# A new order table for a threshold-attention kernel, and one GpSimd drain more

## The chip, the cores and the metric

The kernel runs on one core of a Trainium2 chip. The metric is the device time of one execution in microseconds (us); the time given for a kernel is the median over its runs. A profile is one execution recorded by the hardware profiler, and times within it count from the start of its span.

## The reference

```python
batch, heads, seq, dim = 8, 12, 512, 64          # Q, K, V: float32, threshold 0.1
scores = np.einsum('bhqd,bhkd->bhqk', Q, K) * scale
weights = np.exp(scores - np.max(scores, axis=-1, keepdims=True))
weights = weights / (np.sum(weights, axis=-1, keepdims=True) + 1e-10)
weights = np.where(weights > threshold, weights, 0)
weights = weights / (np.sum(weights, axis=-1, keepdims=True) + 1e-10)
return np.einsum('bhqk,bhkd->bhqd', weights, V)
```

With random inputs nearly every weight is below the threshold, so nearly every row of the output is zero. The kernel makes use of that.

## The kernel before

The output is filled with zeros by 24 large stores (`do_zero`, a *fill* of 512 KB each). The work is to find the few query rows that have a weight above the threshold, and to write those rows.

The 96 heads are taken in 48 pairs, the pairs in 24 *quads*. For a quad, Q and K are loaded (`load_q`, `load_k`), Q is cast to 16 bits (`qcast`, L367 to L371), both are transposed on TensorE (`ktr` L381, `qtr` L410) and taken out of PSUM (`kev` L389/L391, `qev` L416), and K is cast (`kh` L396/L400). Then for each pair and each 128 keys: scores into PSUM (`sc`, L438), an exponential of them (`ex`, on ScalarE L447 or, as a bit trick, on VectorE L449), and sums over keys (`sm`, L468), which give each query two power sums. 384 exponentials of 128x512 run in all. Beside that the squares of Q and K are taken (`bits`, on GpSimd L425, ScalarE L427 or VectorE L429, two steps for a quad) and summed (`norms`, L478): they only serve as a guard, and nothing waits for them but the check at the end.

Pairs form three groups (24, 16 and 8 pairs). When a group's sums are complete, `y`, `d`, `fl` and `mx` on VectorE find the queries whose power sums tell of one large weight. Six *stages* (0 to 5, of 8 pairs; stage 5 is group 2) then finish those queries: `m`, `ix`, `qi` make row numbers; `gq` (L534) gathers the rows of Q by an indirect transfer that GpSimd issues; `xm`, `xev`, `xqk`, `xexp` (L541 to L562) compute their scores again in full precision; `xcut`, `xkeep`, `vi`, `oi` (L566 to L580) find the one key above the threshold; `gv` (L585) gathers that row of V, and `scatter` (L600) writes it to the output. So GpSimd issues 18 indirect transfers: six gq, six gv, six scatters. gv of stage 3 waits for the fills of quads 12 to 23, and each scatter for the fills of its own quads.

Every engine runs its instructions in order. The order is not written out as code: each step is entered in a plan by `add(name, engines, ...)`, and the table `ORDER` lists all 1325 steps as words: the step's number in base 36 and a letter for the engine that takes it (P TensorE, V VectorE, A ScalarE, G GpSimd, S the load queue of SyncE, Q that of ScalarE, N none). `Plan.order` goes through the table and emits each step. A step that has a choice of engines (`ex`, `kev`, `bits`, `xev`, `y`, the casts) takes the one of its letter. Buffers come from pools in the order of the table. The table sets only each engine's own order; at run time an engine waits for data through semaphores. The numbers given to `add` (a cost for each engine, a latency) were used to make such a table and cost nothing on the chip.

Loads and fills are issued on SyncE, at most eight in flight, so a fill stands behind the loads that come before it in the table.

Behind the plan a check counts queries that do not fit the scheme; if there are any, a slow loop (`tc.If(many > 0)`) computes everything in the plain way. With these inputs the branch is not taken. The program ends with a barrier in which each engine drains and SyncE waits for all transfers.

Of the kernel before, what the change touches and what calls it, by code (L numbers as in the profile page):

```python
# [94 lines left out]
def kernel(  # L95
# [18 lines left out]
    nc = tc.nc  # L114
# [391 lines left out]
    def quads_of(x):  # L506
        p0, k = pairs_of_stage(x)
        return range(p0 // 2, (p0 + k) // 2)
# [195 lines left out]
    for g in range(NG):  # L704
# [14 lines left out]
        for x in xs:  # L719
            def xstep(name, engs, lat, after, fn, takes=(), gives=(), mode=None, pr=pr + LAG, x=x):  # L720
                deps = [(a, x) if isinstance(a, str) else a for a in after]
                add((name, x), engs, lat, deps, pr, lambda e: fn(e, x), takes, gives, mode)
# [8 lines left out]
            xstep("xev", {"ACT": 0.3, "DVE": 0.34}, 0.15, ["xm"], do_xev, takes=[("xq", x)],  # L731
                  gives=[("one", ("xm", x))])
            xstep("xqk", {"PE": 1.75}, 0.25, ["xev"], do_xqk, takes=[("one", ("xs", x))],
                  gives=[("xq", x)] + [("big", ("kt", j)) for j in quads_of(x)], mode="c")
            xstep("xexp", {"ACT": 0.7}, 0.12, ["xqk"], do_xexp, takes=[("cut", x)])
            xstep("xcut", {"DVE": 0.15}, 0.04, ["xexp"], do_xcut)
            xstep("xkeep", {"DVE": 0.76}, 0.04, ["xcut"], do_xkeep, gives=[("cut", x), ("one", ("xs", x))])
            xstep("vi", {"DVE": 0.12}, 0.36, ["xkeep"], do_vi)
            xstep("oi", {"DVE": 0.12}, 0.12, ["xkeep", "qf"], do_oi)
            filled = [j for w in range(x, NX) for j in quads_of(w)] if x == NX - 3 else []  # L740
            xstep("gv", {"POOL": 1.25}, 0.1, ["vi"] + [("z", j) for j in filled],
                  lambda e, x, filled=filled: do_gv(e, x, filled), takes=[("vr", x)])
            xstep("scatter", {"POOL": 1.25}, 0.3, ["gv", "oi"] + [("z", j) for j in quads_of(x)], do_scatter)
    bad = consts.tile([P, len(PARTS) + NG + NX], f32)
    nc.vector.memset(bad[:], 0.0)

    NK = len(PARTS)

    def do_check_norm(eng):
        nc.vector.tensor_scalar(bad[:, 0:NK], nmax[:], NORM_CAP / BITS, 0.5, op0=ALU.is_le, op1=ALU.is_lt)  # L750

    def do_check_count(eng):
        for g in range(NG):
            nc.vector.tensor_scalar(bad[HI, NK + g:NK + 1 + g], count[HI, g:g + 1], J * FAR, is_row[HI, g:g + 1],
                                    op0=ALU.is_gt, op1=ALU.mult)
# [19 lines left out]
    Kd, Vd = (t.rearrange("b h (p r) d -> (b h) p (r d)", p=P, r=SO) for t in (K, V))  # L775
    with tc.If(many > 0):
        k_sb, v_sb, q_sb = k_b[0][:, 0, :, 0:D], k_b[1][:, 0, :, 0:D], qs_b[0]
        kt, qt, mt = kt_b[2][0:D, 0, :], kt_b[3][0:D, 0, 0:P], kt_b[4][:, 0, :]
        st, e, m = cut_b[0], kt_b[5][:, 0, :], kt_b[6][:, 0, :]
        with tc.For_i(0, B * H, 1) as hd:  # L780
            nc.sync.dma_start(out=k_sb, in_=Kd[hd].rearrange("p (r d) -> p r d", r=SO))
            nc.sync.dma_start(out=v_sb, in_=Vd[hd].rearrange("p (r d) -> p r d", r=SO))
            for r in range(SO):
                nc.tensor.matmul(one[1][0:D, r * P:(r + 1) * P], lhsT=k_sb[:, r, :], rhs=identity_f32[:],
                                 is_transpose=True, start=True, stop=True)
            nc.scalar.copy(kt, one[1][0:D, :])
            with tc.For_i(0, SO, 1) as r0:
# [58 lines left out]
```

## Time and profile before

| | |
|---|---|
| Median of 3 runs | 172.13 us (171.56 to 172.7) |
| The profiled execution | 173.78 us |
| Its span, first to last instruction | 172.0 us |
| Granted TensorE clock, mean | 0.994 of full |
| Busy in the span: TensorE, VectorE, ScalarE, GpSimd | 160.1, 150.1, 149.4, 130.4 us |
| HBM read and written | 25.56 MB, 12.78 MB |
| Transfers on the load queue of SyncE | 76.1% of 16 DMA engines over the span |

How to read it: busy time is the union of an engine's instructions; register, branch, semaphore and DMA-issuing instructions are not counted. Matmul ends are modelled, so a busy TensorE is not one at its peak. Neighbouring instructions of VectorE, ScalarE and GpSimd overlap by some tens of ns, so a duration is a little longer than the step from one start to the next. An indirect transfer's span on GpSimd is its issue; its data land later.

### The profile page before, as it was taken

The numbers are of one execution on the slowest core, as the hardware profiler recorded it, in microseconds if no ns is written. First come the engines' busy times: TensorE is split into PE (matmuls) and PEld (weight loads), VectorE is DVE, ScalarE is ACT, GpSimd is POOL, SyncE is SP. The second block draws the span as 40 slices with busy tenths as digits, with TensorE's granted clock in tenths as the row PEclk, the third lists the DMA queues.
The fourth block names the chain that finished last, engine by engine and source line by source line (L and its number), as shares of the span: only waits on it lengthen the run. The fifth ranks groups of instructions, "written<-read, shape, count | busy, mean of one in ns | idle before, by whom it ended". The sixth has DMA issues, their size and how long they took to land. (4 is left out here: it accounts for less than half of the span.)

```text
span 172.0 us, 5811 instructions
## 1 busy us (share of the span) xinstructions
PE 160.1 (93%) x2190; PEld 62.7 (36%) x2190; DVE 150.1 (87%) x349; ACT 149.4 (87%) x297; POOL 130.4 (76%) x198
## 2 busy tenths in 40 slices
PE   6598999999999999999999999999999999998950
PEld 2253443443354243434442354334243333332320
DVE  5198999999999999999999999899689999997450
ACT  2577999999999999999999999999899999936720
POOL 8119979999989988960785999799869959536451
PEclk9999999999999999999999999999999999999997
DMA  5999999989899689796998989999899980000000
GB/s 162 263 234 286 238 268 252 278 194 270 184 269 289 143 235 379 166 326 150 226 331 243 320 185 264 360 385 266 268 308 374 398 346 13 1 3 5 6 5 7
DMA packets 67453, 38.27 MB, mean 222 GB/s; under 512 B 51938, under 2 KB 64349, under 8 KB 67424
## 3 DMA queue, kind: packets, MB, share of 16 engines
q1 hardware_dynamic: 64992, 37.10, 76.1%
q10 hardware_dynamic: 1856, 0.66, 1.6%
q8 instruction: 17, 0.28, 0.7%
q0 software_dynamic: 576, 0.13, 0.5%
q14 instruction: 12, 0.10, 0.2%
HBM read 25.56 MB, written 12.78 MB: 223 GB/s over the span
## 5 line engine op out<-in xcount | busy, mean ns | idle before, releaser
L447 ACT ACTIVATE e<-one 128x512 f16<-128x512 f32 x231 | 120.0, 639 | 3.2 <-PE one L438 2.2
L449 DVE TENSOR_SCALAR e<-one 128x512 uint16<-128x512 f32 x153 | 97.0, 683 | 3.3 <-PE one L438 2.9
L438 PE MATMUL one<-big 64*128 64x512 f16 x384 | 67.6, 391 | 1.0 <-ACT big L396 0.5
L468 PE MATMUL sum<-e,w_s 128*32 128x512 f16 (+1 forms) x768 | 59.4, 387 | 0.9 <-ACT e L447 0.7
L425 POOL TENSOR_TENSOR big<-big 128x512 bf16<-128x512 f16 x52 | 52.8, 1038 | 2.3 <-DVE big L429 1.8
L400 POOL CAST big<-big 128x512 f16<-128x512 f32 x47 | 28.2, 613 | 16.3 <-ACT big L389 4.5
L371 POOL CAST qh<-big 128x512 f16<-128x512 f32 x45 | 26.7, 614 | 6.0 <-DMA big<-in_Q_dram 3.0
L438 PEld LDWEIGHTS <-big 64*128 64x128 f16 x384 | 17.2, 97 | 34.5 <-issue 28.1
L468 PEld LDWEIGHTS <-w_s 128*32 128x32 f16 (+1 forms) x768 | 15.9, 95 | 36.1 <-issue 31.5
L389 ACT COPY big<-one 128x512 f32<-128x512 f32 (+1 forms) x37 | 20.5, 591 | 2.7 <-PE one L381 2.6
L416 DVE COPY big<-one 128x512 f16<-128x512 f16 (+1 forms) x52 | 19.5, 398 | 3.3 <-PE one L410 1.2
L381 PE MATMUL one<-identity_f,big 64*128 64x64 f32 x384 | 18.7, 234 | 1.7 <-DMA big<-in_K_dram 1.5
L381 PEld LDWEIGHTS one<-identity_f,big 64*128 64x128 f32 x384 | 16.1, 145 | 6.9 <-issue 3.0
L391 DVE COPY big<-one 128x512 f32<-128x512 f32 (+1 forms) x15 | 9.7, 649 | 3.6 <-PE one L381 3.4
L556 PE MATMUL one<-big,xq 128*32 128x512 f32 x96 | 11.5, 598 | 0.5 <-issue 0.5
L410 PEld LDWEIGHTS <-qh 64*128 64x128 f16 x384 | 9.0, 97 | 7.6 <-issue 3.5
L410 PE MATMUL one<-identity_h,qh 64*128 64x64 f16 x384 | 11.3, 195 | 0.0
L534 POOL DMA_INDIRECT qs<-in_Q_dram,idx x6 | 6.4, 1060 | 6.2 <-DVE idx L524 4.8
L600 POOL DMA_INDIRECT out_dram<-vr,idx x6 | 6.1, 1024 | 4.1 <-DVE cut L566 2.2
L427 ACT ACTIVATE big<-big 128x1024 bf16<-128x1024 f16 x8 | 8.3, 1059 | 0.0
L585 POOL DMA_INDIRECT vr<-in_V_dram,idx x6 | 6.4, 1066 | 2.3 <-DVE idx L575 1.3
L562 ACT ACTIVATE one<-one 128x512 f32<-128x512 f32 x6 | 3.7, 612 | 3.3 <-DVE vals L504 2.0
(83 smaller groups left out, 80.9 us busy)
## 6 DMA issues: line engine op xcount, KB each, us to landing
out_dram<-zero SPq DMA_DIRECT2D x24, 512.0 KB, 6.2
big<-in_K_dram SPq DMA_DIRECT2D x93, 128.0 KB, 4.2
big<-in_Q_dram SPq DMA_DIRECT2D x22, 512.0 KB, 5.5
big<-in_Q_dram SPq DMA_DIRECT2D x3, 256.0 KB
big<-in_K_dram ACTq DMA_DIRECT2D x3, 128.0 KB
big<-in_Q_dram ACTq DMA_DIRECT2D x1, 256.0 KB
qs<-in_Q_dram,idx POOLq DMA_INDIRECT x6
vr<-in_V_dram,idx POOLq DMA_INDIRECT x6, 4.0
```

Source lines behind the costliest of these rows:

```text
L371: behind(nc.gpsimd.tensor_copy(dst, src))
L381: nc.tensor.matmul(dst[i][:, c:c + D], lhsT=src[ps, n0 + n, r, :], rhs=identity_f32[ps, ps], is_transpose=True, start=True, stop=True)
L389: nc.scalar.copy(dst, src)
L400: behind(nc.gpsimd.tensor_copy(dst, src))
L410: nc.tensor.matmul(dst[i][:, c:c + D], lhsT=src[ps, n0 + n, r, :], rhs=identity_h[ps, ps], is_transpose=True, start=True, stop=True)
L416: nc.vector.tensor_copy(qk_b[big("qk", q)][:, 0, n0:n0 + k, i * SO * D:(i + 1) * SO * D], src)
L425: behind(nc.gpsimd.tensor_tensor(out=dst[:, n, :], in0=src[:, n, :], in1=src[:, n, :], op=ALU.mult))
L438: nc.tensor.matmul(one[at("one", ("sc", hp, t, h))][:], lhsT=qk[ps, 1, n, t * P:(t + 1) * P], rhs=qk[ps, 0, n, :], start=True, stop=True)
L447: nc.scalar.activation(dst, src, ACTF.Exp, scale=scale, bias=-11.0 * math.log(2.0))
L449: nc.vector.tensor_scalar(dst.bitcast(u16), src, scale * LOG2E * 1024.0, 4096.0, op0=ALU.mult, op1=ALU.add)
L468: nc.tensor.matmul(dst[32 * j:32 * j + 32, :], lhsT=w, rhs=x, start=first, stop=False, skip_group_check=True)
L556: nc.tensor.matmul(one[at("one", ("xs", x))][sl, :], lhsT=xq_b[at("xq", x)][:, n, sl], rhs=kt_b[big("kt", quads[j])][:, n, :], start=(n == ...
```

## The change

The table `ORDER` is replaced by another one of 1326 words over the same steps and one new step. The new step, `("drain", 0)`, is a `drain` instruction of GpSimd; it comes after `mx` of group 2, and the last scatter depends on it in the plan. Two loads of the slow loop go to ScalarE's queue instead of SyncE's.

```diff
-ORDER = """6N fQ hS 1G gQ 24S 7P 18Q 22S 8P 9P 0G 5V 23S aP 16S 17Q bP cP 2vS dP iA
...
-xqP qqA lcP thN 10mV pfP xjV tiP 10eV 10oG xkN 103V xlP 10rV w8P qrN 10nV 10sV imP qsP ejP jzP 105G xsV 10qV 10pG"""
+ORDER = """2G 0G 22S fQ 6N 7P 8P hS 9P aP 23S 24S 2vS bP gQ cP iA jP 2tS nP 26P kA
...
+xoP 10nV 10oG laA mpP xpP xqP jzP lcP w7N w8P tiP 10tV zuV 103V 105G h9P qsP xlP xsV 10pG uuN 108N lbN s4N 10rV"""
...
-            xstep("scatter", {"POOL": 1.25}, 0.3, ["gv", "oi"] + [("z", j) for j in quads_of(x)], do_scatter)
+            xstep("scatter", {"POOL": 1.25}, 0.3, ["gv", "oi"] + [("z", j) for j in quads_of(x)]
+                  + [("drain", 0)] * (x == NX - 1), do_scatter)
+    add(("drain", 0), {"POOL": 1.95}, 0.0, [("mx", NG - 1)], 999, lambda e: nc.gpsimd.drain())
...
-            nc.sync.dma_start(out=k_sb, in_=Kd[hd].rearrange("p (r d) -> p r d", r=SO))
-            nc.sync.dma_start(out=v_sb, in_=Vd[hd].rearrange("p (r d) -> p r d", r=SO))
+            nc.scalar.dma_start(out=k_sb, in_=Kd[hd].rearrange("p (r d) -> p r d", r=SO))
+            nc.scalar.dma_start(out=v_sb, in_=Vd[hd].rearrange("p (r d) -> p r d", r=SO))
```

Read step by step, the tables differ in these counts. "Body" is from an engine's first exponential to its last; a full `kev` is 512 columns wide, a half one 256.

| Steps | before | after |
|---|---|---|
| ScalarE, body: ex / kev full / kev half / bits / Q cast / y | 231 / 31 / 5 / 2 / 0 / 1 | 236 / 27 / 3 / 0 / 1 / 0 |
| VectorE, body: ex / kev full / kev half / bits / Q cast / y / constants | 153 / 13 / 1 / 9 / 1 / 1 / 0 | 148 / 17 / 3 / 4 / 0 / 2 / 1 |
| GpSimd, ahead of the last ex: bits / gq / gv / scatter | 26 / 4 / 3 / 2 | 24 / 3 / 3 / 0 |
| behind the last ex: bits on VectorE / on ScalarE | 5 / 6 | 13 / 7 |
| fills behind the last K load on SyncE | 9 | 14 |
| score steps (`sc`, of 192) ahead of the last K load in the table | 155 | 166 |

The constants are `const_base`, a row of small VectorE steps that stood first on VectorE and now stands behind 132 other steps of it. The constants of GpSimd (masks, index rows) are moved too. Behind its last cast or square, GpSimd's order is

```
before: scatter1 gq3 gq4 scatter2 gq5 gv3 scatter3 gv4 gv5 scatter4 scatter5
after:  gq3 scatter0 gq4 scatter1 gq5 drain gv3 scatter2 gv4 scatter3 gv5 scatter4 scatter5
```

(before, scatter1 and gq3 stand among the last exponentials). Around the end of the body, VectorE's and TensorE's orders of the steps that lead to the last gq are

```
before, VectorE: bits y2 qi4 d2 fl2 mx2 m5 qi5 ...   TensorE: ... ix4 xm3 norms8 norms19 xqk3 ix5 xm4 xqk4 xm5 ...
after,  VectorE: bits qi4 y2 d2 fl2 mx2 m5 qi5 ...   TensorE: ... xm3 xqk3 ix5 xm4 norms8 norms16 xqk4 xm5 ...
```

The loads at the start are reordered as well: before, the first halves of quads 0 and 1 come first (with the second half of quad 0 among them), then the second half of quad 1; after, the first half of quad 0 and both halves of quad 1, then the K of quad 2, then the second half of quad 0.

## Rows read from the trace of the kernel before

**Rows 1.** Busy us by stretch: PE, PEld, DVE, ACT, POOL; clock, DMA share, GB/s.

```profile
20.00:80.00 60.00, 60.00 (x938) 24.20 (x934) 58.23 (x106) 59.43 (x121) 52.30 (x91) 1.00 0.94 248
80.00:150.00 70.00, 69.23 (x938) 25.85 (x935) 65.77 (x138) 68.01 (x138) 56.71 (x73) 1.00 0.83 265
150.00:172.00 22.00, 15.32 (x166) 5.94 (x165) 12.24 (x41) 9.58 (x17) 10.01 (x10) 0.95 0.03 5
```

**Rows 2.** Timeline (start us, us, what, count) of repeated steps; one early stretch.

```profile
86.97 1.07 ACT L389 COPY big<-one 128x512 f32<-128x512 f32 x2
...
141.86 6.13 ACT L447 ACTIVATE e<-one 128x512 f16<-128x512 f32 x12
...
143.68 0.68 DVE L449 TENSOR_SCALAR e<-one 128x512 uint16<-128x512 f32 x1
...
149.34 1.88 DVE L449 TENSOR_SCALAR e<-one 128x512 uint16<-128x512 f32 x3
...
2.00:3.60 1.60, 1.60 (x20) 0.63 (x16) 1.54 (x23) 0.25 (x1) 1.59 (x3) 1.00 0.99 272
```

**Rows 3.** Timeline of the tail.

```profile
153.29 1.92 PE L556 MATMUL one<-big,xq 128*32 128x512 f32 x16
...
155.31 0.38 PE L519 MATMUL one<-ones,m 64*128 64x1 f32 x2
...
156.29 1.02 POOL L534 DMA_INDIRECT qs<-in_Q_dram,idx  x1 [0.94 <-DVE cut L566]
...
156.59 2.01 ACT L427 ACTIVATE big<-big 128x1024 bf16<-128x1024 f16 x2
...
157.12 0.75 DVE L429 TENSOR_SCALAR big<-big 128x512 int32<-128x512 int32 x2
...
157.62 1.21 POOL L585 DMA_INDIRECT vr<-in_V_dram,idx  x1 [0.31 <-issue]
...
158.29 0.42 DVE L429 TENSOR_SCALAR big<-big 128x512 int32<-128x512 int32 x1
...
160.35 1.05 ACT L427 ACTIVATE big<-big 128x1024 bf16<-128x1024 f16 x1
...
164.21 1.00 POOL L585 DMA_INDIRECT vr<-in_V_dram,idx  x1 [0.85 <-DVE idx L575]
...
167.55 0.99 POOL L600 DMA_INDIRECT out_dram<-vr,idx  x1 [0.91 <-issue]
```

**Rows 4.** Timeline around two gathers; in brackets idle time before and releaser.

```profile
107.30 0.41 PE L410 MATMUL one<-identity_h,qh 64*128 64x64 f16 x16
...
107.62 1.06 POOL L534 DMA_INDIRECT qs<-in_Q_dram,idx  x1
...
108.89 0.60 ACT L447 ACTIVATE e<-one 128x512 f16<-128x512 f32 x1 [0.38 <-PE sum L468]
108.89 0.42 DVE L416 COPY big<-one 128x512 f16<-128x512 f16 x1 [0.70 <-PE sum L468]
...
119.96 0.40 PE L410 MATMUL one<-identity_h,qh 64*128 64x64 f16 x16
...
120.39 1.06 POOL L585 DMA_INDIRECT vr<-in_V_dram,idx  x1 [0.16 <-issue]
...
121.21 0.95 DVE L416 COPY big<-one 128x512 f16<-128x512 f16 x2 [0.58 <-PE one L410]
```

**Rows 5.** Drains at the end: ns min/median/max, first and last start us.

```profile
L841 POOLq DRAIN  x3: 45/107/1611, 169.5 to 171.7; - x3
L841 SPq DRAIN  x3: 7/7/13, 170.6 to 171.4; - x3
```

**Rows 6.** Landing of the gathers of V, from their issue.

```profile
DMA to landing us min/median/max: 2.6/4.0/5.4
```

**Rows 7.** Busy us by stretch around the last fills, columns as in rows 1.

```profile
130.00:140.00 10.00, 9.80 (x144) 3.62 (x140) 9.78 (x18) 9.95 (x21) 8.16 (x9) 1.00 1.00 389
140.00:150.00 10.00, 9.87 (x128) 3.13 (x121) 9.75 (x21) 9.79 (x20) 7.64 (x10) 1.00 0.16 60
```

2 lines of the change are left out of this document (1 added, 1 removed).

## The prediction

> **What bounds the kernel now.** I first read the table of stretches, to see which engine leaves no room where. TensorE is shown as busy throughout, but its ends are modelled, so the busy share says little about it; ScalarE and VectorE are the ones to look at. In the 130 us from 20 to 150 ScalarE is busy 59.43 + 68.01 = 127.4 us and VectorE 58.23 + 65.77 = 124.0 us [rows 1]. Idle is left there for 2.6 us on ScalarE and 6.0 us on VectorE. These two engines empty every PSUM tile, so up to the last exponential ("the body"; it ends at 149.34 + 1.88 = 151.2 [rows 2]) their summed work sets the time. From 150 to 172 it is otherwise: of 22 us VectorE is busy 12.2, ScalarE 9.6 and GpSimd 10.0 [rows 1]. There a chain is in charge: last sums, index of the largest scores, gather of query rows (gq), dot products (xqk), exponentials, gather of value rows (gv), scatter. I read that chain in the timeline. The last gq starts at 156.29, the last gv at 164.21, the last scatter at 167.55, and the span ends at 172.0 [rows 3]. So gq to gv is 7.92 us, gv to scatter 3.34 us, and from the last scatter to the end 4.45 us.
>
> So the change has two places to act: work on ScalarE and VectorE before the last exponential, and the order on GpSimd behind it.
>
> **Part 1: work shared out anew.** The counts come from the two tables, read word by word with the step numbers (front part). What one more instruction costs is its start-to-start time, not its duration, for neighbours overlap. Rows of several instructions give it: (duration of the row minus that of one) over the number of further ones. ScalarE's exponential: 12 in 6.13 us, one 0.60 [rows 4], so (6.13 - 0.60)/11 = 0.50 us. VectorE's: 3 in 1.88 us, one 0.68, so 0.60 us. A full K eviction on ScalarE: 2 in 1.07 us, one near the exponential's 0.60, so 0.47 us; on VectorE I take 0.60 as for the exponential, the same 128x512 out of PSUM [rows 2]. A norm square on ScalarE: 2 in 2.01 us, one 1.05: 0.96 us; on VectorE 2 in 0.75 us, one 0.42: 0.33 us [rows 3].
>
> Between first and last exponential, ScalarE: 5 exponentials more (+2.5), 4 full K evictions fewer (-1.9), 2 half ones fewer (an estimate of 0.27 each from 0.47 for the full one, -0.5), 2 squares fewer (-1.9), a Q cast more and the clipping y fewer (each near 0.55 as the other 512-column steps, 0): -1.8 us. VectorE: 5 exponentials fewer (-3.0), 4 full K evictions more (+2.4), 2 half ones more (+0.7), 5 squares fewer (-1.65), Q cast fewer and y more (0), and the constants of const_base, which filled VectorE's 1.54 busy us between 2.0 and 3.6 when there was no score yet [rows 2], now among the exponentials: +1.5. That is -0.05 us. An exponential may go to either engine, so what counts is the mean: **-0.9 us**. Bounds: -0.05 (VectorE alone decides) and -1.8.
>
> The squares that leave the body run behind the last exponential, 13 on VectorE instead of 5 and 7 on ScalarE instead of 6. I cost them at nothing: VectorE is idle some 10 of the last 22 us and ScalarE 12 [rows 1], and 8 x 0.33 = 2.7 us fits. Without that cover they would cost those 2.7 us. Two squares fewer on GpSimd also cost nothing and gain nothing: it has 13 us of idle time from 80 to 150 [rows 1].
>
> **Part 2: signals of TensorE held back.** At 107.62 GpSimd issues a gather. The transposes of Q at 107.30 are over at 107.71, yet the VectorE copy that reads them starts at 108.89, after 0.70 us of idle time, and ScalarE starts at the same 108.89 after 0.38 us. At 120.39 it happens again: VectorE waits 0.58 us for transposes that end at 120.36, until 121.21, here with the issue not quite over [rows 4]. Both engines wake at once, at 108.89, 0.2 us behind the end of the issue, which speaks for a signal that was late and not for work that was late. So far the trace bears the change's premise out. It is not the whole rule, though: the other six transfers of the body stand beside no idle time that ends so plainly with the issue. Sum: VectorE 1.28 us, ScalarE 0.38 us, mean 0.83. The new table moves scatters 0 and 1 out of the body, leaving six indirect transfers in it (three gq, three gv) of eight, and places the rest with the delay counted. Bounds: 0 and 0.83; I take all of it, since the gaps are few and the order around them is free to change: **-0.8 us**.
>
> **Part 3: the tail on GpSimd.** Between the last gq and the last gv there were three indirect transfers (gv, scatter, gv); now there are a drain, gv3, scatter2, gv4 and scatter3. Each issue takes 1.0 us, one 1.2 [rows 3], with 0.3 us ahead of it in the row at 157.62. The trace has no drain in such a place. Nearest: the three drains of GpSimd at the end, 0.045, 0.107 and 1.61 us, of which the long one is the first behind the indirect transfers [rows 5]. I take 1.61 for the new one, as it stands behind 11 of them. Then GpSimd needs 1.0 + 0.1 + 1.6 + 4 x 1.3 + 0.3 = 8.2 us from the last gq to the last gv, where the chain needs 7.92: **+0.3 us**. With a drain of 0.1 us it would be 0; with one that waits until the gather in front of it has landed, 2.6 us from its issue in the empty tail [rows 6], no more than the 2.7 above; with the 5.4 us of a loaded one, +3. Queued behind the drain are gv3 and all later transfers, so each of its microseconds beyond 1.3 is passed on.
>
> In return the drain at the end has seven transfers behind it rather than eighteen. GpSimd's long drain ends at 169.5 + 1.6 = 171.1, SyncE comes to its first drain at 170.6 [rows 5]. If the long drain shrinks, SyncE is last: **-0.45 us**, bounds 0 and -0.5. What runs before the last gq (y, d, fl, mx, m, ix, qi) keeps its order; scatter1 now stands where scatter2 stood. The slow path's loads move from SyncE to ScalarE inside a branch that is not taken: 0.
>
> **Part 4: start and fills.** The loads are put in another order, first exponential near 8.8 as before: 0, bounds -0.7 and +0.7. On SyncE 14 fills of the output stand behind the last K load instead of 9. Five fills of 512 KB at 389 GB/s are 5 x 1.35 = 6.7 us. Before, the transfers filled the engines to 140 and 16% of the next ten, so they ended near 141.6 [rows 7]; now near 148.3. I cost that at nothing because the first gather of the tail that matters is issued near then. It is what the third rival is about.
>
> The DMA engines take from several rings in turn, a packet each, says the Trainium skill (DMA: Bandwidth & Descriptors, section on queues, rings and completion order). By that a gather issued beside fills queues among them, and the trace agrees: gathers of V landed between 2.6 us, in the empty tail, and 5.4 us, in the loaded body [rows 6].
>
> **Sum.** -0.9 - 0.8 + 0.3 - 0.45 = -1.85 us. The profiled span of 172.0 becomes 170.15; that execution took 173.78 us, 1.78 around its span, and would take 171.9. The runs' median is 172.13, near the span, so I forecast 172.13 - 1.85 = **170.3 us**.
>
> **Rivals.**
> *More of the body's idle time goes.* Of the 2.6 and 6.0 us [rows 1], mean 4.3, 0.8 is in the sum. A new order may take half of the rest, 1.75 us: 168.5. For it: a whole new table. Against: the gaps left are small and scattered.
>
> *The signals are held as before* (the change doesn't do what it says). The -0.8 falls away: 171.1. For it: six transfers stay in the body, and only two of eight left a trace, so placing by that rule may miss what decides.
>
> *Fills reach the first gather.* If the fills still run when gq3 is issued, it lands up to 5.4 - 2.6 = 2.8 us later [rows 6]. Its xqk (153.29 to 155.21) stands ahead of the last ix on TensorE, which started at 155.31, right behind it [rows 3], so lateness is passed on, less some 0.7 us by which gq3 may go earlier (one more exponential behind its index, 0.60, and some order): about +1.5 us, 171.8. It begins when the fills end after some 147.
>
> *Fills reach the last gather: slower.* The last K load stands behind 166 of the 192 score steps instead of 155; if it really comes 11/192 of the 142 us from the first exponential (near 9) to the last later, 8 us, the fills end near 156 and gq5 too lands late: +1.5 + 2.8 = 4.3, 174.6. It decides from an end of the fills near 156.
>
> *Squares block GpSimd.* The gv at 157.62 took 1.21 us with two VectorE squares beside it, the others 1.0 [rows 3]. With 13 squares beside the transfers, up to five would be 0.2 us longer: +1.0, 171.3. The Trainium skill (SBUF — State Buffer, section on the two separate sides) says that a VectorE operation in a two-port mode locks GpSimd out of writing descriptors until it ends. By that rule the same squares speak against this change; the row shows 0.2 us of it.
>
> **Chances.** Forecast 0.42 (169.6 to 171.0, more than half of it under 170.4); more idle gone 0.20; held as before 0.10; first gather late 0.14; last gather late 0.09; squares 0.05. A measurement here can tell about 1%, so faster means under 170.4: 0.25 of the forecast, 0.20, and a little of the others, 0.48. Slower, over 173.9: the last gather late and a part of the first, 0.12. Same: 0.40. The range leaves out the slow case and the lower half of the second: 167.6 to 172.6.
>
> **What would show it.** Right: the last exponential ends near 149.5; no idle over 0.3 us of VectorE or ScalarE behind a TensorE signal beside an indirect transfer; a GpSimd drain near 1.6 us ahead of gv3 and a final one well under 1; last gq to last gv near 8.2 us; DMA empty by 149. Wrong: one that ends at 151 (parts 1 and 2), an xm for gq3 more than 3 us behind its issue (fills), a drain over 2.5 us, gaps of 0.5 us left in the body.

## The result and the profile after

| | before | after |
|---|---|---|
| Median | 172.68 us (171.56 to 173.03, 13 runs) | 173.87 us (173.05 to 174.6, 13 runs) |
| Ratio, 95% interval | | 1.0077 [1.0054, 1.0101] |
| The profiled execution, its span | 173.78 us, 172.0 us | 173.87 us, 172.1 us |

The change made the kernel 0.8% slower, 1.2 us. The forecast was 170.3 us, 1.8 us under the median, with a range up to 172.6. The two profiled spans are equal, but the profiled execution of before lies 1.1 us above its median and that of after on its median, so before was profiled a second time (b1, fifth set).

Changed kernel, busy time by stretch, columns as in [rows 1]. The first row is the body, from the first exponential to the end of the last.

```profile
8.28:150.10 141.82, 138.88 (x2001) 54.98 (x2000) 134.69 (x286) 136.00 (x275) 113.27 (x170) 1.00 0.91 257
...
20.00:80.00 60.00, 59.15 (x882) 23.41 (x882) 58.39 (x108) 59.20 (x120) 52.96 (x78) 1.00 0.87 231
80.00:150.00 70.00, 68.62 (x987) 27.47 (x984) 65.89 (x157) 66.04 (x135) 52.41 (x68) 1.00 0.91 280
...
140.00:150.00 10.00, 10.00 (x139) 3.82 (x136) 9.85 (x21) 9.88 (x20) 6.66 (x8) 1.00 0.86 335
```

Of the 130 us from 20 to 150, ScalarE is busy 59.20 + 66.04 = 125.2 us and VectorE 58.39 + 65.89 = 124.3; in [rows 1] it was 127.4 and 124.0. So these 130 us have 1.9 us more idle time than before (the two engines together), not less. The fills keep the transfers busy for 0.86 of the ten us from 140, so they end near 148.6 (an estimate).

Changed kernel, timeline. First gaps in the body (in brackets: idle time before, and who ended it), then the tail.

```profile
24.60 0.76 DVE L416 COPY big<-one 128x512 f16<-128x512 f16 x2 [1.06 <-ACT e L447]
...
100.30 1.04 PE L556 MATMUL one<-big,xq 128*32 128x512 f32 x8
...
101.73 0.69 DVE L449 TENSOR_SCALAR e<-one 128x512 uint16<-128x512 f32 x1 [1.05 <-PE one L438]
...
107.21 1.92 PE L556 MATMUL one<-big,xq 128*32 128x512 f32 x16
...
109.25 0.58 ACT L562 ACTIVATE one<-one 128x512 f32<-128x512 f32 x1 [0.85 <-PE one L556]
...
109.74 2.48 DVE L449 TENSOR_SCALAR e<-one 128x512 uint16<-128x512 f32 x4 [0.69 <-PE one L438]
...
113.95 1.92 PE L556 MATMUL one<-big,xq 128*32 128x512 f32 x16
...
116.03 0.58 ACT L562 ACTIVATE one<-one 128x512 f32<-128x512 f32 x1 [0.70 <-PE one L556]
...
116.48 0.69 DVE L449 TENSOR_SCALAR e<-one 128x512 uint16<-128x512 f32 x1 [0.90 <-PE one L438]
...
148.22 1.89 DVE L449 TENSOR_SCALAR e<-one 128x512 uint16<-128x512 f32 x3
...
154.83 1.03 POOL L534 DMA_INDIRECT qs<-in_Q_dram,idx  x1 [1.22 <-DVE idx L524]
...
158.95 1.02 POOL L585 DMA_INDIRECT vr<-in_V_dram,idx  x1 [3.08 <-DVE cut L566]
...
160.27 1.29 POOL L600 DMA_INDIRECT out_dram<-vr,idx  x1 [0.30 <-DVE idx L575]
...
164.52 1.03 POOL L585 DMA_INDIRECT vr<-in_V_dram,idx  x1 [0.30 <-DMA vr<-in_V_dram,idx]
...
167.72 0.99 POOL L600 DMA_INDIRECT out_dram<-vr,idx  x1 [0.85 <-DVEq L778]
```

The last exponentials end at 148.22 + 1.89 = 150.11, 1.1 us earlier than in [rows 2]; gq5 is issued 1.46 us earlier than in [rows 3]. By gv5 the lead is gone (164.52 after 164.21). GpSimd stands idle for 3.08 us between gq5 and gv3, and from gv3 to gv5 it issues back to back, with 0.3 us between transfers.

Changed kernel, the two lines with drains of GpSimd (ns min/median/max, first and last start us).

```profile
L745 POOLq DRAIN  x1: 3202/3202/3202, 154.6 to 154.6; - x1
...
L843 POOLq DRAIN  x3: 51/113/2343, 168.6 to 171.8; - x3
L843 SPq DRAIN  x3: 7/7/13, 171.2 to 171.5; - x3
```

The new drain takes 3.20 us, from 154.61 to 157.81; the final one, 1.61 us in [rows 5], takes 2.34 us, from 168.57 to 170.91.

### The profile page after: what moved, and what is told of

Read it like the earlier page. It is cut to its first block, busy times and chain, and to the rows that moved or that the text cites. A ratio compares the mean times of both kernels' runs of the same rounds, so it can differ in the third digit from the quotient of the medians.

```text
span 172.1 us, 5828 instructions
## 1 busy us (share of the span) xinstructions
PE 157.8 (92%) x2190; PEld 62.3 (36%) x2190; DVE 150.3 (87%) x354; ACT 147.4 (86%) x292; POOL 128.0 (74%) x196
## 5 line engine op out<-in xcount | busy, mean ns | idle before, releaser
L447 ACT ACTIVATE e<-one 128x512 f16<-128x512 f32 x236 | 121.5, 636 | 4.3 <-PE one L438 3.8
L449 DVE TENSOR_SCALAR e<-one 128x512 uint16<-128x512 f32 x148 | 94.0, 682 | 5.1 <-PE one L438 4.6
L438 PE MATMUL one<-big 64*128 64x512 f16 x384 | 66.3, 385 | 2.2 <-DVE big L416 1.1
L468 PE MATMUL sum<-e,w_s 128*32 128x512 f16 (+1 forms) x768 | 58.4, 384 | 0.4 <-DVE y L495 0.3
L425 POOL TENSOR_TENSOR big<-big 128x512 bf16<-128x512 f16 x48 | 48.6, 1039 | 2.2 <-DVE m L513 2.0
L438 PEld LDWEIGHTS <-big 64*128 64x128 f16 x384 | 17.4, 95 | 38.6 <-issue 31.1
L416 DVE COPY big<-one 128x512 f16<-128x512 f16 (+1 forms) x52 | 18.5, 395 | 2.3 <-ACT e L447 1.1
L389 ACT COPY big<-one 128x512 f32<-128x512 f32 (+1 forms) x31 | 17.3, 593 | 1.5 <-PE one L381 1.3
L391 DVE COPY big<-one 128x512 f32<-128x512 f32 (+1 forms) x21 | 13.1, 630 | 4.3 <-PE one L381 4.3
L556 PE MATMUL one<-big,xq 128*32 128x512 f32 x96 | 11.5, 598 | 0.6 <-ACT xq L547 0.5
L600 POOL DMA_INDIRECT out_dram<-vr,idx x6 | 6.8, 1132 | 2.4 <-issue 0.9
L427 ACT ACTIVATE big<-big 128x1024 bf16<-128x1024 f16 x7 | 7.1, 1051 | 0.0
```

What stands on the lines that cost most here:

```text
L389: nc.scalar.copy(dst, src)
L391: nc.vector.tensor_copy(dst, src)
L416: nc.vector.tensor_copy(qk_b[big("qk", q)][:, 0, n0:n0 + k, i * SO * D:(i + 1) * SO * D], src)
L425: behind(nc.gpsimd.tensor_tensor(out=dst[:, n, :], in0=src[:, n, :], in1=src[:, n, :], op=ALU.mult))
L438: nc.tensor.matmul(one[at("one", ("sc", hp, t, h))][:], lhsT=qk[ps, 1, n, t * P:(t + 1) * P], rhs=qk[ps, 0, n, :], start=True, stop=True)
L447: nc.scalar.activation(dst, src, ACTF.Exp, scale=scale, bias=-11.0 * math.log(2.0))
```

## The experiments

The runs came in five sets after the first; the kernels of a set share the runs of the kernel before. In two of the sets (the first two below) VectorE and ScalarE started late behind TensorE work that they waited for ("late signals" below; the last section says what this leaves open), in the three others they did not. The kernel before was 1 us slower there (173.87 and 173.76 us, otherwise 172.68 to 172.90) and the changed kernel 5 us. So kernels are compared within a set, or between sets of the same kind.

**First set: the drain and the fills.**

```diff
e1_no_drain, e3_drain_late and e4_thin_fills against the changed kernel:
-    add(("drain", 0), ..., lambda e: nc.gpsimd.drain())
+    add(("drain", 0), ..., lambda e: None)                          # e1
- gq5 drain gv3 scatter2 gv4 scatter3 gv5 scatter4 scatter5
+ gq5 gv3 scatter2 gv4 scatter3 gv5 scatter4 drain scatter5          # e3, in the table
-        inst = issuer(eng).dma_start(out=Oz[q], in_=zero[:])
+        inst = issuer(eng).dma_start(out=Oz[q][0:1], in_=zero[0:1])  # e4, the last 14 fills
e2_before_drain against the kernel before, in do_gq behind the transfer:
+        if x == NX - 1:
+            nc.gpsimd.drain()
```

> The changed kernel without its drain; the table of order is otherwise the same. Theory A (the drain is the loss): in the changed kernel it kept GpSimd from 154.61 to 157.81, and gv3, ready at 156.1, started at 158.95, so that gv5 came at 164.52 where its index was ready at 162.5 and its turn would have been near 162.8. Without it gv5 should start about 8.0 us behind gq5 and the median should fall by 1.5 to 1.9 us, to 172.0 to 172.4. Theory B (the table is the loss: its body and its order on the other engines): gv5 starts earlier but the end does not move, median 173.3 to 174.0.

> The kernel before with one GpSimd drain added right behind the last gq, and nothing else. Theory A: the drain ends only when the gather in front of it has landed, 3 us behind its issue, near 159.5; gv3 moves from 157.62 to 159.9, the scatter behind it waits for its landing until 162.9, gv4 164.2, gv5 165.5 instead of 164.21: median up by 1.0 to 1.5 us, and the final drain is no shorter. Rival (the sum of the prediction: a drain of 1.6 us, and a final drain that shrinks because fewer transfers stand behind it): gv5 within 0.3 us of before and 0.45 us gained at the end, median between -0.5 and +0.1 of before.

> The changed kernel with its drain moved from behind the last gq to between the last two scatters. If a drain lasts until the transfer in front of it is through (theory A), gv5 comes near 162.8 as without a drain, the drain then holds the last scatter until some 3.2 us behind the start of the scatter before it, near 167.4, where it could start near 166.0: median 1.2 to 1.6 us above the kernel without the drain, and the final drain is again 2 us or more. If a final drain's length goes by the number of transfers since the last drain (the reason why the prediction took 0.45 us off the end), it now has one behind it and falls to under 0.5 us, and the time is near that of the kernel without a drain or below.

> The changed kernel with the 14 fills behind the last K load cut to one partition row of each (the other rows of these blocks are left unwritten, that is left out). Theory of the fills (third rival of the prediction): gq3 lands late because the fills run until 148.6; its xm started 3.19 us behind the issue where before it was 2.46. Then xm of gq3 comes back to about 2.5 us and the median falls by 0.5 to 0.8 us. Theory that they cost nothing in the time: ScalarE and VectorE set the order up to the last gq whatever gq3 does, median within 0.3 us of the changed kernel.

Measured, before 173.87 us: e1 177.28 us (ratio 1.0173), e2 176.07 (1.0117 [1.0080, 1.0155]), e3 178.45 (1.0240), e4 179.55 (1.0300). All four were above what any theory gave. For e1, e3 and e4 the reason is that the changed kernel itself was slower here, which only the next set showed (179.06 us). Against that, taking out the drain gained 1.8 us and moving it ahead of the last scatter gained 0.6 us; adding it to the kernel before cost 2.2 us. These are the sizes of theory A, but e1's tail was not as told: gq5 to gv5 was 9.29 us, not 8.0, because the copy after xm5 started 1.24 us behind its matmuls, beside the issue of scatter2. In e2 it was 9.84 us, as theory A had it, and e3's final drain took 2.33 us with only one transfer behind the earlier drain: it waited for that transfer, the last scatter, and ended 0.08 us behind its landing at 175.43. Thin fills gained nothing (0.5 us worse, with late signals in both). The transfers were empty by 130 instead of 148, yet xm3 started 2.72 us behind gq3's issue in e4 and 2.73 behind it in c1, with the fills. So the fills did not delay gq3.

**Second set: the changed kernel again, the tail, and the body without transfers.** n1 and n2 skip the eight transfers of stages 0 to 2 in `do_gq`, `do_gv` and `do_scatter`.

```diff
e5_lean_tail against the changed kernel, no drain, and in the table:
- gv0 ... gq3 scatter0 gq4 scatter1 gq5 drain gv3 scatter2 gv4 scatter3 gv5
+ gv0 scatter2 scatter1 ... gq3 scatter0 gq4 gq5 gv3 scatter3 gv4 gv5
n1_after_no_body, n2_before_no_body:
+        if x < 3:            # do_gq, do_gv; x in (0, 1) in do_scatter
+            return
```

> The changed kernel, unaltered, as the measure for the kernels beside it. If its time hangs on the table alone: 1.2 us above the kernel before, as in the first set of runs. If it hangs on when its loads land (in the profiles of the three kernels made from it, the first K eviction came 0.4 us later than in its own profile, and the lateness had grown to 2.3 us by the last score steps, while the kernel before with a drain lost nothing): 2 us or more above before, and the last group's y near 153 instead of 150.6.

> The changed kernel without its drain, with the scatters of stages 1 and 2 issued behind the last body gather (where GpSimd has 2 us of idle time) instead of behind gq4 and gv3, and scatter3 ahead of gv4 as in the kernel before: between gq5 and gv5 stand only gv3, scatter3 and gv4. Theory A2 (what stands on GpSimd between gq5 and gv5 is the loss, the drain or the signals that a scatter there holds back): gq5 to gv5 is 7.9 to 8.4 us again (9.7 in the changed kernel, 9.3 without its drain), and the median falls 1.2 to 2.0 us below the changed kernel beside it. Theory B (the loss is in the body or comes from other engines in the tail): gq5 to gv5 stays over 9 us or the two scatters cost in the body what they save behind it; median within 0.5 us of the changed kernel.

> The changed kernel without the eight transfers of stages 0 to 2 that its table could put beside TensorE's work: the gathers of query and value rows of these stages and scatters 0 and 1 are left out (their buffers stay zero). The body is read from the first exponential to the last group's y, 142.3 us in the changed kernel's profile. If the table does count the held signals (part 2 of the prediction right): there is nothing left to gain, body shorter by 0 to 0.3 us. If it doesn't: shorter by 0.8 us or more.

> The kernel before with the same eight transfers left out. Its body is 143.0 us. If held signals cost it what part 2 of the prediction took from the gaps at 108.89 and 121.21 (mean 0.83 us): 142.0 to 142.3. If such gaps are covered by the other engine's work or by slack, within 0.3 us of 143.0, and part 2 had nothing to win. If other places suffer too: under 141.7.

Measured, before 173.76 us: c1 179.06 us (1.0293 [1.0245, 1.0342]), e5 176.76 (1.0143 [1.0091, 1.0195]), n1 176.61 (1.0152), n2 173.74 (0.9993 [0.9956, 1.0030]). The lean tail brought gq5 to gv5 back to 7.95 us and 2.3 us of time. The two kernels without body transfers are read from their bodies:

Changed kernel again (c1), its body and its timeline around gq2 and gq4.

```profile
8.99:152.69 143.70, 139.96 (x2001) 55.27 (x2000) 135.24 (x286) 136.46 (x275) 113.57 (x170) 0.99 0.89 253
```

```profile
102.79 1.02 POOL L534 DMA_INDIRECT qs<-in_Q_dram,idx  x1
...
102.94 0.40 PE L410 MATMUL one<-identity_h,qh 64*128 64x64 f16 x16
...
104.28 0.76 DVE L416 COPY big<-one 128x512 f16<-128x512 f16 x2 [0.64 <-PE one L410]
...
153.42 1.03 POOL L534 DMA_INDIRECT qs<-in_Q_dram,idx  x1 [0.71 <-DVE idx L524]
154.11 0.69 DVE L488 TENSOR_SCALAR y<-sum 64x512 f32<-64x512 f32 x1 [0.96 <-PE one L541]
...
154.85 0.37 ACT L547 COPY xq<-one 128x256 f32<-128x256 f32 x1 [1.57 <-PE one L541]
```

Changed kernel without the transfers (n1): body, and the gaps in it.

```profile
9.97:151.97 142.00, 139.20 (x2001) 55.30 (x2000) 134.86 (x286) 135.91 (x275) 105.85 (x162) 1.00 0.89 255
```

```profile
103.60 0.69 DVE L449 TENSOR_SCALAR e<-one 128x512 uint16<-128x512 f32 x1 [1.05 <-PE one L438]
...
111.11 0.58 ACT L564 ACTIVATE one<-one 128x512 f32<-128x512 f32 x1 [0.85 <-PE one L558]
...
111.60 2.48 DVE L449 TENSOR_SCALAR e<-one 128x512 uint16<-128x512 f32 x4 [0.69 <-PE one L438]
...
117.89 0.58 ACT L564 ACTIVATE one<-one 128x512 f32<-128x512 f32 x1 [0.70 <-PE one L558]
...
118.35 0.69 DVE L449 TENSOR_SCALAR e<-one 128x512 uint16<-128x512 f32 x1 [0.90 <-PE one L438]
```

Kernel before without the transfers (n2): body.

```profile
8.80:149.25 140.45, 139.25 (x1998) 55.28 (x1996) 135.40 (x267) 137.44 (x278) 108.36 (x169) 0.98 0.91 258
```

Idle time in a body is its length less the busy time, as a mean of VectorE and ScalarE. c1: 143.70 - (135.24 + 136.46)/2 = 7.9 us. n1: 142.00 - (134.86 + 135.91)/2 = 6.6. n2: 140.45 - (135.40 + 137.44)/2 = 4.0. In the changed kernel's own profile, shown above: 141.82 - (134.69 + 136.00)/2 = 6.5. So in that profile the transfers cost the new body nothing (6.5 with, 6.6 without), while in c1 they cost 1.2 us: at 104.28 VectorE's copy starts 0.9 us behind its transposes, beside gq2 (and behind the body, at 154.11, y waits beside gq4). But the new order has 2.6 us more idle time than the old one with none of these transfers in either (6.6 against 4.0), at the same five places in n1 as in the changed kernel (1.05, 0.85, 0.69, 0.70, 0.90 us).

n2's body is 2.4 us shorter than that of e2 (142.82 us, the kernel before with its transfers in a late set), yet its median is that of the kernel before: in its profile gq5 to gv5 took 9.32 us, 1.4 more than in the recorded one. Why was not traced.

**Third set: moving the transfers that signals met.**

```diff
e6_gq2_later, e7_gq4_behind, e8_lean_both (e5 with the edits of e6 and e7):
- gq2 bits9,0            + bits9,0 gq2                   # e6, e8
+        if x == 4:                                       # e7, e8, in do_gq
+            tc.add_manual_dep(inst.ins, evs[3].ins.name, ...)   # behind the copy after xm3
```

> The changed kernel, unaltered, once more as the measure for the three kernels beside it. If this chip is like the one before: 3.0% over the kernel before, with late signals at 104 us (0.6 us of idle VectorE), at the last group's y (1.0 us) and at the last norm maximum. If it is like that of the first set of runs: 0.8% over, and none of the three.

> The changed kernel with gq2 moved behind the norm square that followed it on GpSimd, 2.1 us later; nothing else. In the repeat of the changed kernel gq2 was issued from 102.80 to 103.82, and the VectorE copy of Q's transposes, done on TensorE at 103.34, started at 104.28. Theory of held signals: the copy now starts within 0.1 us of its transposes, that idle time (0.6 us) is gone unless another signal meets the later issue, and the last gq's come 0.5 to 0.9 us earlier against the changed kernel beside it: median 0.3 to 0.9 us lower. Theory that TensorE itself is late there (its ends are modelled): the gap stays, time within 0.2 us.

> The changed kernel with one wait added: gq4 is issued behind the ScalarE copy that follows xm3 instead of as soon as its index is there, some 0.5 to 1.0 us later. In the repeat of the changed kernel the last group's y started at 154.11, 0.96 us after its sums were through on TensorE, and the copy after xm3 1.13 us after its matmuls, both beside the issue of gq4 (153.42 to 154.45). Theory of held signals: y starts within 0.1 us of its sums, the copy within 0.1 us of xm3, and everything behind, gq5 first, comes 0.8 to 1.0 us earlier; median 0.6 to 1.2 us lower, though a wait was added. Theory that a wait only costs: time the same or up to 1 us higher.

> The changed kernel without its drain and with scatters 1 and 2 in the body (gq5 to gv5 was 7.95 us that way), with gq2 later and gq4 behind the copy after xm3. If the effects add: 2.3 + 0.6 + 0.9 = 3.8 us below the changed kernel beside it, on a chip like the last one near 175.2, on one like the first near 172. If the held signals only move to other places: 2.3 us below and no more.

Measured, before 172.90 us: c2 174.30 us (1.0079 [1.0049, 1.0109]), e6 174.42 (1.0088), e7 174.51 (1.0089), e8 174.47 (1.0089). No signal was late in this set, so e6 and e7 had nothing to mend; e7's wait cost 0.5 us between y and gq5 (4.66 us after 4.15 in c2) and 0.2 us in the median, which is not told from none. In e8 gq5 to gv5 was 8.37 us, but the added wait took 0.8 us of it back ahead of gq5 (y to gq5 4.96 us) and the end another 0.9 (5.16 us after the last scatter), so the time stayed; the gains did not add. Whether a late signal can be mended by moving a transfer stays open. Changed kernel again (c2), the places that were late in c1:

```profile
103.07 1.02 POOL L534 DMA_INDIRECT qs<-in_Q_dram,idx  x1 [0.15 <-issue]
...
103.84 0.74 DVE L416 COPY big<-one 128x512 f16<-128x512 f16 x2
...
152.10 0.68 DVE L488 TENSOR_SCALAR y<-sum 64x512 f32<-64x512 f32 x1
152.34 1.03 POOL L534 DMA_INDIRECT qs<-in_Q_dram,idx  x1 [0.72 <-DVE idx L524]
```

The same instructions with the same distances: here the copy starts 0.77 us behind the start of gq2 with no idle time, in c1 1.49 us behind it after 0.64 us.

**Fourth set: the drain and the tail without late signals, and transfers moved in the kernel before.** e9, e10 and e11 are e1, e5 and e2 again.

```diff
e12_before_moved against the kernel before, in the table:
- bits15,0 gq2 ... gv0 ... qcast21,1 ... gv1 ... gv2
+ gq2 bits15,0 ... qcast21,1 gv0 ... gv2 gv1
```

> The changed kernel without its drain, once more; the changed kernel itself stands at 1.008 of before where no signals are late and at 1.029 where they are (which of the two this is shows in the body's length, 142.3 or 145 us). Theory A (the drain on GpSimd is the loss): gq5 to gv5 falls from 9.5 to about 8.0 us where no signal is late, the end gives 0.3 us of it back through a longer final drain: ratio 0.998 to 1.002, or 1.018 with late signals. Theory B (the drain keeps GpSimd quiet while xm5's signal is on its way, so that a held signal takes the place of the wait): gq5 to gv5 stays over 9 us, ratio 1.005 to 1.010.

> The changed kernel without its drain and with scatters 1 and 2 in the body, once more. Theory A2 (what stands on GpSimd between gq5 and gv5): gq5 to gv5 near 8.0 us, last group's y as in the changed kernel, ratio 0.996 to 1.001 where no signal is late. If scatters in the body cost there what they save behind it: y 0.5 to 1.0 us later, ratio 1.003 or more.

> The kernel before with one drain behind the last gq, once more. It cost 2.1 us (1.012) where the kernel made from the change had late signals, with gq5 to gv5 up from 7.93 to 9.84 us. Theory A: the same here, 1.009 to 1.014, for nothing in it hangs on late signals. Otherwise under 1.005.

> The kernel before with three transfers moved and nothing else: gq2 ahead of the two norm squares that stood before it on GpSimd (from 107.6 to about 105.4), gv0 behind the next three casts (from 120.4 to about 125.7, where GpSimd was idle), gv1 behind gv2 (from 122.6 to about 138.8). If the idle time at 108.89 (0.70 and 0.38 us), 121.21 (0.58) and 122.75 (0.47) is theirs and can be won by moving them, as part 2 of the prediction had it: these gaps are gone, body 0.6 to 0.9 us shorter, ratio 0.994 to 0.997. If they meet other signals there: the same idle time in other places, ratio 0.998 to 1.002.

Measured, before 172.70 us: e9 173.35 us (1.0039 [1.0009, 1.0069]), e10 173.35 (1.0033 [1.0007, 1.0059]), e11 173.82 (1.0058 [1.0028, 1.0087]), e12 173.98 (1.0062 [1.0032, 1.0093]). The changed kernel without its drain (e9), gq5, gv3, gv5 and the last scatter:

```profile
155.34 1.03 POOL L534 DMA_INDIRECT qs<-in_Q_dram,idx  x1 [1.12 <-DVE cut L566]
...
156.68 2.00 POOL L585 DMA_INDIRECT vr<-in_V_dram,idx  x1 [0.31 <-issue]
...
163.41 1.03 POOL L585 DMA_INDIRECT vr<-in_V_dram,idx  x1 [0.30 <-DMA vr<-in_V_dram,idx]
...
166.84 0.99 POOL L600 DMA_INDIRECT out_dram<-vr,idx  x1 [1.07 <-DVE many_f L770]
```

The kernel before with a drain (e11), gq5, gv3, gv5, the last scatter, and the drain:

```profile
154.22 1.03 POOL L534 DMA_INDIRECT qs<-in_Q_dram,idx  x1 [0.94 <-DVE cut L568]
...
158.38 0.99 POOL L587 DMA_INDIRECT vr<-in_V_dram,idx  x1 [3.14 <-issue]
...
164.15 1.00 POOL L587 DMA_INDIRECT vr<-in_V_dram,idx  x1 [0.31 <-issue]
...
167.37 0.98 POOL L602 DMA_INDIRECT out_dram<-vr,idx  x1 [0.33 <-issue]
```

```profile
L539 POOLq DRAIN  x1: 3282/3282/3282, 154.0 to 154.0; - x1
```

Without the drain gq5 to gv5 is 8.07 us (9.69 with it). With it the kernel before needs 9.93 us (7.92 without). So the drain costs the step 1.6 to 2.0 us. In the time it is less, 0.65 us (1.0077 to 1.0039, with intervals that overlap) and 1.0 us (1.0058), because the end gives some back: the last scatter to the end is 4.83 us in e9 and 4.38 with the drain, 4.36 in e11 and 4.93 without one (b1, below). Even without its drain the changed kernel is slower than before, by 0.4% with an interval that is clear of 1 by 0.1%. The scatters of the tail (e10 after e9) make no difference. e12 shows what the body is like to touch. With three transfers moved its idle time is 141.90 - (135.82 + 137.58)/2 = 5.2 us, by the row below; in e11 beside it, where they stand as before, the body is 140.56 us with 3.9 us of idle time.

```profile
8.73:150.63 141.90, 139.58 (x1998) 55.23 (x1996) 135.82 (x267) 137.58 (x278) 116.96 (x177) 1.00 0.91 256
```

**Fifth set: the kernel before once more, and a drain where GpSimd waits anyway.** b1 is unaltered.

```diff
e13_drain_in_wait against the kernel before, in do_gv behind the transfer:
+        if x == NX - 3:
+            nc.gpsimd.drain()
```

> The kernel before, unaltered, profiled once more. If the two gaps belong to its order: they are there again, body near 143.0 us. If they come and go with late signals and the profile on which the prediction rests caught an execution that had them: body near 141.2 us, no idle time of 0.5 us at 108.9 and 121.2, idle time of VectorE and ScalarE in the body near 4.6 and 3.1 us instead of 6.65 and 4.72.

> The kernel before with one drain behind gv3, where GpSimd waits 2.6 us for that gather's landing anyway before scatter3 (157.62 to 161.02). If a drain lasts until the transfer in front of it is through: it takes some 3.2 us from gv3's issue, scatter3 starts within 0.3 us of where it did, gq5 to gv5 stays at 7.9 to 8.3 us, and the time from the last scatter to the end falls from 4.9 to about 4.3 us: ratio 0.996 to 1.000. If a drain costs its length wherever it stands: gq5 to gv5 over 9.5 us, ratio 1.004 or more.

Measured, before 172.72 us: b1 172.95 us (1.0000 [0.9970, 1.0030]), e13 172.10 (0.9966 [0.9934, 0.9997]). The kernel before again (b1), body and timeline:

```profile
9.98:150.62 140.64, 139.34 (x1998) 55.29 (x1996) 135.96 (x267) 137.45 (x278) 116.81 (x177) 1.00 0.89 257
```

```profile
108.44 1.06 POOL L534 DMA_INDIRECT qs<-in_Q_dram,idx  x1 [0.15 <-issue]
...
108.93 0.41 DVE L416 COPY big<-one 128x512 f16<-128x512 f16 x1
...
120.44 1.06 POOL L585 DMA_INDIRECT vr<-in_V_dram,idx  x1 [0.16 <-issue]
120.75 0.82 DVE L416 COPY big<-one 128x512 f16<-128x512 f16 x2
...
155.69 1.02 POOL L534 DMA_INDIRECT qs<-in_Q_dram,idx  x1 [0.95 <-DVE cut L566]
...
163.78 1.00 POOL L585 DMA_INDIRECT vr<-in_V_dram,idx  x1 [0.59 <-DVE idx L575]
...
167.07 0.99 POOL L600 DMA_INDIRECT out_dram<-vr,idx  x1 [0.63 <-DVE many_f L768]
```

The gaps of [rows 4] are not there. The copy that started 1.27 us behind its gather there starts 0.49 us behind it here (108.93 after 108.44), and the one at 121.21 has no idle time in front of it (120.75). The body is 140.64 us instead of 142.38, its idle time 140.64 - (135.96 + 137.45)/2 = 3.9 us instead of 5.7. The gaps are absent in e11 and e13 too, whose order is the same up to gq5 (bodies of 140.56 and 140.96 us), and present in e2: two of five profiles have them. b1 ran on the same chip as the two sets with late signals, and there e2 had a body of 142.82 us. So it is not the chip.

e13 beats both kernels, by 0.3% with an interval that all but reaches 1. Its drain lasted 3.50 us and cost nothing, as expected: gq5 to gv5 is 162.80 - 154.67 = 8.13 us. But the end was not shortened (171.0 - 166.05 = 4.95 us after the last scatter), and from the first exponential on no part of its profile is shorter than in b1 by more than 0.05 us; its first exponential came at 8.65 us, b1's at 9.98. So where the 0.6 us of the medians come from is not shown.

## Why the prediction was wrong

Two steps failed. The first is that the body shrinks with the summed work of VectorE and ScalarE, and by the gaps beside two gathers. It was forecast 1.7 us shorter; it came 1.2 us longer than in b1, which has none of those gaps, because its idle time rose by 2.6 us. The second is the size of the drain: +0.3 us was forecast from gq5 to gv5, and 1.6 came.

The terms, in us, each from one profile: the profile on record, the kernel before again (b1), the changed kernel.

| stretch | record | b1 | after | forecast | after - b1 |
|---|---|---|---|---|---|
| start to first exponential | 8.84 | 9.98 | 8.28 | 0 | -1.7 |
| first to last exponential | 142.38 | 140.64 | 141.83 | -1.7 | +1.2 |
| to gq5 | 5.07 | 5.07 | 4.72 | 0 | -0.3 |
| gq5 to gv5 | 7.92 | 8.09 | 9.69 | +0.3 | +1.6 |
| gv5 to last scatter | 3.34 | 3.29 | 3.20 | 0 | -0.1 |
| last scatter to the end | 4.45 | 4.93 | 4.38 | -0.45 | -0.5 |
| whole span | 172.0 | 172.0 | 172.1 | -1.85 | +0.1 |

The three spans are alike, but the start varies by itself: the first exponential came between 8.2 and 10.0 us in the profiles, whatever the kernel. From the first exponential on the difference is +1.8 us; the medians say +1.2, and single profiles of one kernel differ by some tenths in each stretch. The body's figure repeats: 140.6, 140.6 and 141.0 us in the three profiles of the old order without the gaps (b1, e11, e13), 141.8 to 142.1 us in the seven of the new one without late signals (the changed kernel, c2, e6 to e10).

**What bounds the kernel.** Right in part: the tail goes by the chain and GpSimd. The body is the work of ScalarE and VectorE and their waits for TensorE, and the waits were read as the kernel's own, 5.7 us in the profile on record, of which 1.7 were not there in b1.

**Part 1, work shared out anew: right in size, and the larger term missed.** The mean busy time of the two engines in the body fell from 136.7 (b1) to 135.35 us, 1.35 us less; forecast 0.9, bounds 0.05 and 1.8 (ScalarE 1.45 less after 1.8, VectorE 1.27 less after 0.05). The step that failed is the one behind it, that the body follows the summed work. Its idle time went from 3.9 to 6.5 us. The rival "more of the body's idle time goes" had the place right and the sign wrong: a whole new table may lose idle time as well as win it, and the prediction gave only the winning side a case. Where it is lost can be read from the gaps. Three times in the body TensorE does the 16 dot-product matmuls of a stage (L556, ending at 101.3, 109.1 and 115.9; of the first the row above shows the last eight). At 109 and 116 us ScalarE waits for them (0.85 and 0.70 us), and each time VectorE waits for scores that stand behind them on TensorE (1.05, 0.69 and 0.90 us, by L438). In b1 the largest gaps of that kind are 0.27 and 0.47 us. Of the gaps over 0.25 us, the changed kernel has some 1.7 us more there than b1 (mean of the two engines) and some 1.0 us more before 30 us, where the loads stand in another order too (1.06 at 24.60 is the largest). That these placements cause the gaps is read from the rows, not tested; that the order has them without any transfer of the body is shown by n1.

**Part 2, signals held back: wrong.** The 0.8 us were taken from gaps at two gathers in the profile on record. That execution took 173.78 us, 1.65 over the median of 172.13. The prediction worked out 171.9 for the execution itself and then took the same 1.85 us off the median; but gaps of one execution need not be in the others, and three of the five profiles of this order have none of them. b1's body is 1.7 us shorter than the recorded one: the two gaps that part 2 counted are half of it (0.83), and most of the rest are a pair near 16.4 us (0.46 and 0.50, which e13 has too) and a pair near 125 that is twice as long as in b1 (0.68 and 0.68 after 0.34 and 0.27). The time of an execution does not tell this by itself: b1's took 173.78 us as well, for it started 1.1 us later and ended 0.5 us more slowly. In an execution without the gaps there was nothing to win, as n2 shows as well (4.0 us of idle time without the transfers, 3.9 with them in b1). The rival "signals held as before" was near, but it took the premise for granted: it said that the gaps stay, not that they are often absent.

**Part 3, the tail: the drain was mis-sized, the end nearly right.** It lasted 3.20 us, not 1.61. The prediction had the right alternative in hand (it waits for the gather in front) and costed it at 2.7 us from gq5 to the end of the drain; that came as 157.81 - 154.83 = 2.98. What it left out is that gv3 started only at 158.95, 1.14 us behind the drain's end (in e3, e11 and e13 the next transfer came 0.9 to 1.1 us behind it) and 4.12 us behind gq5, and that four issues then took 5.57 us (one of 1.29 beside four VectorE squares), not 5.2.

A drain's length had two parts. One is the wait: gq5 landed at 157.31, and the drain ended 0.50 us behind that. The other goes by the number of transfers since the drain before, as the prediction took it to: the drains that had to wait ended 0.08 us behind the landing of the transfer ahead with one such transfer (e3), 0.25 with five (e13, last), 0.33 with seven (changed kernel, last), 0.50 with 11, 0.54 with 12 (e11), 0.58 with 13 (e13) and 0.78 with 18 (b1, last), so some 0.04 us for each. Where the last transfer had landed before the final drain began, that drain took 0.69 us with seven (c1) and 1.61 with 18 (e1):

```profile
L843 POOLq DRAIN  x3: 51/107/694, 175.2 to 176.8; - x3
...
L843 POOLq DRAIN  x3: 45/107/1611, 173.5 to 175.7; - x3
```

The end gained 0.55 us after 0.45. The final drain is not under 1 us but 2.34, since it waits for the last scatter. SyncE is last, as told: it comes to its first drain at 171.2, when GpSimd's has ended at 170.91 (in b1 GpSimd's ended at 171.15, behind SyncE's 171.0). But from the landing of the last scatter to the end it is 1.51 us instead of 1.63 in b1, so this explains 0.12 us. The rest is that the scatter landed 2.86 us behind its start instead of 3.30, which was not forecast and has no cause that the runs show, so the near hit is partly luck. Moved to where GpSimd waits anyway (e13) a drain cost nothing.

**Part 4, start and fills: right.** They ended near 148.6 (148.3 forecast). xm3 came 3.19 us behind gq3's issue, over the mark of 3 that the prediction set, but in c1 and c2, with the same fills, it came 2.73 us behind it, and in e4, with the fills gone by 130, 2.72.

**The other rivals.** The fills did not reach the last gather (it landed 2.48 us behind its start). Squares beside an issue lengthened one by 0.3 us (1.29 at 160.27, four squares), like the one in [rows 3]. The Trainium skill (SBUF — State Buffer, section on the two separate sides) says that a VectorE operation in a two-port mode keeps GpSimd from writing descriptors; this row agrees with it. So does e9, where the drain no longer stands beside the squares and gv3's issue took 2.00 us beside six of them. But in e1 gv3 took 1.06 us beside three, and the longest issue of the changed tail, 1.45 us at 152.16, has no square beside it, so what the squares cost is not settled, and no run shows the mode in which they run.

## What to carry to other kernels

A gap in a profile is worth its length only if other executions have it too: look for it in a second profile of the same kernel before counting it as something to win. A changed order moves idle time as well as work, and here it was the larger term: 1.35 us of work less and 2.6 us of idle time more. A drain costs what GpSimd would otherwise have issued until the transfer in front of it has landed, and about a microsecond behind that, so its place is behind a transfer that must be waited for anyway.

## What the runs showed of the hardware

A GpSimd drain directly behind an indirect transfer took 3.1 to 3.5 us in the tail (3.20 in the changed kernel, 3.15 in e3, 3.28 in e11, 3.50 in e13) and 2.78 in n1, against some 1.0 us for the transfer's issue. It ended 0.5 to 0.6 us behind the landing of that transfer with 11 to 13 transfers since the drain before, 0.17 behind it with three (n1).

Beside an indirect transfer's issue VectorE and ScalarE sometimes start late behind the TensorE work that they wait for (1.1 us in c1, 1.2 in e1, 1.8 in e4), in the profiles of two sets and in the recorded one, and not in others, on the same chip too (e2 has it and b1 not). In these two sets the kernel before was 1 us slower and the changed one 5 us; in c1, 1.9 us of that lie in the body and 1.8 behind the last scatter. The Trainium skill (Perfetto Trace Analysis, section on the Tensor Engine instruction) says that TensorE's end times in a trace are worked out from the instruction's size; so whether the signal is late or the matmuls are cannot be told from these rows, and what brings the lateness on stays open.
